# Hybrid decoder layer on one core: the extra 32 rows of an expert multiplied for four weight chunks in one block instead of two

## The chip, the cores and the metric

One core of one Trainium2 chip runs one launch of the kernel. The metric is device microseconds (us) of that launch. Engines: PE is TensorE (PEld its weight loads), DVE VectorE, ACT ScalarE, POOL GpSimd, SP SyncE, whose queue carries most of the loads.

## The reference

One decoder layer over 1024 rows of 1024 columns: pooling and attention, a mixture of experts, a gated projection of `p`, a final norm. The change is in the mixture:

```python
logits = hf @ w_router + b_router            # 1024 rows, 32 experts
topv, topi = lax.top_k(logits, 4)
gates = softmax(topv)
# for each expert e, on the rows xb that chose it:
gu = xb @ w_gate_up[e] + b_gate_up[e]        # 1024 -> 2048
g, u = minimum(gu[:, :1024], 7), clip(gu[:, 1024:], -7, 7)
y = ((u + 1) * g * sigmoid(1.702 * g)) @ w_down[e] + b_down[e]   # 1024 -> 1024
out[row] += gate * y
# behind it
x = x + (p @ w_ple_proj) * sigmoid(rmsnorm(x) @ w_ple_gate)
```

## The kernel before

After the attention part the kernel runs through 32 experts, sorted by their number of rows and interleaved so that large and small ones alternate. Each expert has 128 "main" rows. The 18 large ones, those with `REM[s] = 1` (s counts in processing order), have up to 32 "further" rows as well.

**Chunks.** An expert's weights come as 12 chunks of 1 MB: eight gate-up chunks g0 to g7 (128 rows of `w_gate_up`) and four down chunks d0 to d3 (256 rows of `w_down`). The order is g0..g7 of expert s, then d0..d3 of expert s-1, then g0..g7 of expert s+1, and so on. One pass of the loop (over c, the chunk's number) handles one chunk. Passes are called by their chunk here: "pass g5".

**Main rows.** A chunk lands in a tile `raw`. ACT copies each half to `wh` at reduced precision and DVE forms the rest `wl` (`split`, L104 and L105); pass c splits chunk c+2. PE then makes three products for every 512 columns (`mm3`, L99 to L101), 12 matmuls for a chunk, into `gu` or `d`.

**Further rows.** Their 32 columns fill a quarter of the array's columns, so four products run side by side in the four column groups, in plain float32 straight from `raw`, into a PSUM tile `r` of one buffer. `gu_rem` (L1029) does so for gate-up and `down_rem` (L1085) for down. A group of four products is two instructions each in the trace. Before, `gu_rem` runs in passes g0, g2, g4 and g6 and takes two chunks each time; in g0 it also puts four bias products ahead (L1024). `down_rem` runs in d0 and d2 and takes two chunks. Such a run of instructions is called a block here: six blocks for a large expert, 108 in all.

**What stands between.** Pass g1 transposes the activations of expert s-1 (`a_main`, L979, into `ah` and `al`), g2 the same for its further rows (`a_rem`, L991), g4 and g5 transpose the rows of expert s+1 (`x_main`, L979; `x_rem`, L991), g3 builds one-hot tiles of expert s+2 on DVE, g6 has PE pick its row lists from them (L895, read by small DVE instructions from L916 on). `act_rem` (ACT L1039 and L1040, then DVE) evaluates the gate of the further rows in g6, `act_all` that of the main rows in g7. Output of expert s-2 leaves in g0 (`y_out`).

**Order.** Every engine executes in the order in which the code is written, with waits on semaphores. SP issues the loads in order; a load waits until the former content of its buffer has been split and, for a large expert, multiplied:

```python
for c, (kind, s, k) in enumerate(chunks[:nmain]):
    load_chunk(c + LOADS)          # LOADS = 5, five raw buffers
    ...                            # split(c + 2)
    gu_chunk(s, k, c)
    gu_rem(s, k, c)
```

So the load of chunk c+5 goes into the buffer of chunk c. Behind the loop `p` is read into `pall`, turned and multiplied, and the norms and gates of the eight row tiles follow.

Of the kernel before, what the change touches and what calls it, by code (L numbers as in the profile page):

```python
# [21 lines left out]
D = 1024  # L22
# [49 lines left out]
def layer(ctx, tc, x, p, g_mix, w_in, w_pool, pool_scale, rel_bias, w_out, g_ffn, w_router,  # L72
# [694 lines left out]
    mo_p = tc.tile_pool(name="mo", bufs=1, side="left", reuse_waits="tile")  # L767
    mo = mo_p.__enter__()

    for name in ("al", "ah", "xl", "xh"):  # L770
        mo.tile([128, NK, 128], F32R, name=name, bufs=2)
    for name in ("xr", "atr"):
        mo.tile([128, 256], F32, name=name, bufs=3)
    count(NT - 1)
# [12 lines left out]
    perm2 = rt.tile([128, NE], F32, name="perm2")  # L787
    dve.tensor_scalar(perm2, rank_row, rank, None, op0=OP.is_equal)
    bdb = f3.tile([128, 4, NE], BF, name="bdb")
    bdf = mo.tile([128, D], F32, name="al", bufs=2)[:, :128]  # L790
    with nc.allow_low_precision(reason="zeros and ones"):
        dve.tensor_tensor(bdb, perm2[:, None, :].to_broadcast([128, 4, NE]),
                          maskq[:, :, None].to_broadcast([128, 4, NE]), OP.mult)
# [29 lines left out]

    def onehots(s):
        w = 128 + 128 * REM[s]
        oh = mo.tile([128, NT, 256], BF, name="oh", bufs=1) if s else mo.tile([128, NT, 256], BF, name="ah", bufs=2)
        for i in range(NT):
            dve.tensor_scalar(oh[:, i, :w], slots[:, :w], place[:, i, s:s + 1], None, op0=OP.is_equal)
        S[s]["oh"] = oh
        sel = mo.tile([96, 128], BF, name="sel", bufs=4)  # L830
        dve.tensor_copy(sel, perm2[:96, s:s + 1].to_broadcast([96, 128]))
        S[s]["sel"] = sel
# [32 lines left out]
    def load_chunk(c, after=None, columns=slice(0, 2048)):  # L865
        kind, s, k = chunks[c]
        if c not in raws:
            raws[c] = wp.tile([128, 2048], F32, name="raw", bufs=5)
        if after is not None:
            after.memset(raws[c][:, columns][:, :1], 0.0)  # L870
        if kind in "jp":
            src = w_ple_gate[k * 256:(k + 1) * 256, :] if kind == "p" else w_ple_proj
            sp.dma_start(raws[c].rearrange("p (k c) -> p k c", k=2), src.rearrange("(k p) c -> p k c", p=128))
            return
        if s not in expert:
            expert[s] = sp.value_load(order[0:1, s:s + 1], min_val=0, max_val=NE - 1)
        e = expert[s]
        if kind == "g":
            sp.dma_start(raws[c][:, columns],
                         w_gate_up[ds(e, 1), k * 128:(k + 1) * 128, columns].rearrange("a p c -> p (a c)"))  # L880
        else:
            sp.dma_start(raws[c].rearrange("p (k c) -> p k c", k=2),
                         w_down[ds(e, 1), k * 256:(k + 1) * 256, :].rearrange("a (k p) c -> p (a k) c", p=128))
# [68 lines left out]
    def gates_turned():  # L952

        t = psM.tile([128, 2, 128], F32, name="r", bufs=1)
        for b in range(2):
            pe.transpose(t[:, b, :], gates[:, 4 * b:4 * b + 4, :].rearrange("p i e -> p (i e)"), ident)
        gT = mo.tile([128, D], F32, name="ah", bufs=2)[:, :256]
        act.activation(gT, t.rearrange("p b c -> p (b c)"), AF.Copy)
        t = psM.tile([128, 2, 128], F32, name="r", bufs=1)
        for b in range(2):  # L960
            pe.matmul(t[:, b, :], gT[:, 128 * b:128 * b + 128], bdf, start=True, stop=True)
        return t
# [9 lines left out]

    def turned(src, names):

        hi, lo = (mo.tile([128, NK, 128], F32R, name=n, bufs=2) for n in names)
        for b in range(2):
            t = psM.tile([128, 4, 128], F32, name=f"d{b}", bufs=1)
            for k in range(4):
                pe.transpose(t[:, k, :], src(4 * b + k), ident)  # L979
            split(hi[:, 4 * b:4 * b + 4], lo[:, 4 * b:4 * b + 4], t)  # L980
        return hi, lo
# [33 lines left out]
    def gu_rem(s, k, c):  # L1015


        if not REM[s] or k % 2:
            return
        if k == 0:  # L1020
            S[s]["gur"] = psM.tile([128, 512], F32, name="r", bufs=1)
            table = bgu.rearrange("e (g j c) -> e g j c", g=2, j=4)
            for j in range(4):
                pe.matmul(S[s]["gur"][32 * j:32 * j + 32, :], S[s]["sel"][:, :32], table[:, :, j, :],  # L1024
                          start=True, stop=False)
        for kk in (k, k + 1):
            raw = raws[c + kk - k].rearrange("p (g j c) -> p g j c", g=2, j=4)
            for j in range(4):
                pe.matmul(S[s]["gur"][32 * j:32 * j + 32, :], S[s]["xr"][:, kk, :], raw[:, :, j, :],  # L1029
                          start=False, stop=(kk == NK - 1))  # L1030
# [44 lines left out]
                    k == 0, k == NK - 1)  # L1075

    def down_rem(s, kp, c):
        if not REM[s] or kp % 2:
            return
        if kp == 0:  # L1080
            S[s]["dr"] = psM.tile([128, 256], F32, name="r", bufs=1)
        for k in range(2 * kp, 2 * kp + 4):
            raw = raws[c - kp + k // 2].rearrange("p (k c) -> p k c", k=2)
            for j in range(4):
                pe.matmul(S[s]["dr"][32 * j:32 * j + 32, :], S[s]["atr"][:, k, :],  # L1085
                          raw[:, k % 2, 256 * j:256 * j + 256], start=(k == 0), stop=(k == NK - 1))
# [13 lines left out]
            add_rows(acc4, S[s]["idx", 1], y)  # L1100
        S[s].clear()

    LOADS, SPLITS, TURN0, AT = 5, 4, (4, 7), 8
    load_chunk(0, columns=slice(1024, 2048))

    lists(0, gates=False)
# [33 lines left out]
        split(pT[i][0], pT[i][1], t[:, :2, :])  # L1140

    for c, (kind, s, k) in enumerate(chunks[:nmain]):
        load_chunk(c + LOADS)
        if kind == "g" and k == 0 and s > 1:
            y_out(s - 2)
        if (s, k) != (0, NK - 1):
            for n in range(2 * c + SPLITS, 2 * c + SPLITS + 2):
                split_half(n)
        if kind == "g":
            gu_chunk(s, k, c)  # L1150
            gu_rem(s, k, c)
            if k == NK - 2:
                act_rem(s)
            if k == NK - 1:
                act_all(s)
                if s == 0:
                    for n in range(2 * c + SPLITS, 2 * c + SPLITS + 2):
                        split_half(n)
            if s:
                if k == 1:  # L1160
                    a_main(s - 1)
                if k == 2:
                    a_rem(s - 1)
            if s + 1 < NE:
                if k == 4:
                    x_main(s + 1)
                if k == 5:
                    x_rem(s + 1)
            if s == 0 and k == GK:
                m = psM.tile([128, 2, 2, 6], F32, name="m", bufs=1)  # L1170
                for a in range(2):
                    pick_rows(m[:, a], a, slice(3, 6))
                for a in range(2):
                    slot_gates(m[:, a], a)
                spill_blocks()
            if s == 0 and k == YK:
                for n in range(2):
                    add_rows(acc, rows[:, n:n + 1], ys[n])
            if s + 2 < NE:
                if k == 3:  # L1180
                    onehots(s + 2)
                if k == 6:
                    lists(s + 2)
        else:
            down_chunk(s, k, c)
            down_rem(s, k, c)
            if s == NE - 2 and k == 3:
                pall = mo.tile([128, NT, 256], F32, name="pall", bufs=1)
                act.dma_start(pall, p.rearrange("(i t) c -> t i c", t=128))
                y_out(s)  # L1190
                a_main(NE - 1)
                a_rem(NE - 1)
            if s == NE - 1 and k in (1, 2):
                turn_p(k - 1)
# [84 lines left out]
            dve.scalar_tensor_tensor(r, a, c, r, op0=OP.subtract, op1=OP.mult)  # L1279
        return r  # L1280

    def gain(name, bufs, row):
        g = mo.tile([128, D], F32, name=name, bufs=bufs)
        act.dma_start(g, row_bc(row, D))
        pool.tensor_scalar(g, g, -1.0 / 8192, None, op0=OP.mult)
        return g

    gt = [psM.tile([128, 512], F32, name=f"gu{b}", bufs=1) for b in range(4)]
    gple = gain("oh", 1, g_ple)
    pj, x2, yn, hT = {}, {}, {}, {}  # L1290

    def products(i, n, hi_lo, ws, between=None):
# [15 lines left out]

    def proj(i):
        if i % 2 == 0:  # L1310
            pj[i] = wp.tile([128, 2048], F32, name="raw", bufs=5)
            pj[i], pj[i + 1] = pj[i][:, :D], pj[i][:, D:]
        ps = products(i, 2, pT.pop(i), [parts[2 * nmain + k] for k in range(2)])
        if i + 2 < NT:
            turn_p(i + 2)
        act.activation(pj[i][:, :512], ps[0][0], AF.Copy)
        dve.tensor_copy(pj[i][:, 512:], ps[1][0])

    def load_x2(i):
        name, n = (("xg", 2), ("xg", 2), ("al", 2), ("ah", 2), ("ah", 2))[i % 5]  # L1320
        x2[i] = mo.tile([128, D], F32, name=name, bufs=n)
        sp.dma_start(x2[i], acc[i * 128:(i + 1) * 128, :])

    def squares(i, ss):
# [59 lines left out]
    early(2)  # L1384
    for n in range(2 * nmain + 8, 2 * nmain + 10):
        split_half(n)
    gfin = gain("al", 2, g_final)

    for i in range(NT):
        if i + 4 < NT:  # L1390
# [35 lines left out]
```

## Time and profile before

| | |
|---|---|
| median of 3 runs | 2009.97 us (2009.75 to 2012.18) |
| profiled execution, its own time | 2010.02 us |
| span of its instructions | 2008.3 us |
| PE busy | 1953.4 us, 97% |
| DVE busy | 1502.0 us, 75% |
| ACT busy | 1201.9 us, 60% |
| data moved | 502.18 MB, mean 250 GB/s |

The span is the time from the first to the last profiled instruction; 1.7 us of the run lie outside it. The expert loop takes up about 511 to 1880 us of the span. A matmul's busy time includes its way through the array, so successive ones overlap: from one to the next is read from their starts.

### The profile page before, as it was taken

The numbers are of one execution on the slowest core, as the hardware profiler recorded it, in microseconds if no ns is written. First come the engines' busy times: TensorE is split into PE (matmuls) and PEld (weight loads), VectorE is DVE, ScalarE is ACT, GpSimd is POOL, SyncE is SP. The second block draws the span as 40 slices with busy tenths as digits, with TensorE's granted clock in tenths as the row PEclk, the third lists the DMA queues.
The fourth block names the chain that finished last, engine by engine and source line by source line (L and its number), as shares of the span: only waits on it lengthen the run. The fifth ranks groups of instructions, "written<-read, shape, count | busy, mean of one in ns | idle before, by whom it ended". The sixth has DMA issues, their size and how long they took to land. (4 is left out here: it accounts for less than half of the span.)

```text
span 2008.3 us, 30266 instructions
## 1 busy us (share of the span) xinstructions
PE 1953.4 (97%) x11172; PEld 1429.9 (71%) x11173; DVE 1502.0 (75%) x2464; ACT 1201.9 (60%) x1722; POOL 302.9 (15%) x229
## 2 busy tenths in 40 slices
PE   7999999997999999999999999999999999999998
PEld 6778766775677676677776676776766776766786
DVE  5342575657888797888887887887978787977676
ACT  4222565445667676676676666666766676766533
POOL 0000121302122020212021211120202120201200
PEclk9999999998999999999999999999999999999999
DMA  4421222237898898898897888898987988988711
GB/s 147 126 83 32 85 64 77 93 116 273 324 326 333 293 355 290 304 328 328 307 349 273 310 333 319 312 345 287 353 301 287 335 329 297 351 288 289 241 65 53
DMA packets 117369, 502.18 MB, mean 250 GB/s; under 512 B 12560, under 2 KB 28944, under 8 KB 84576
## 3 DMA queue, kind: packets, MB, share of 16 engines
q1 hardware_dynamic: 99920, 451.46, 59.0%
q0 software_dynamic: 12960, 39.33, 8.6%
q10 hardware_dynamic: 4336, 9.40, 1.5%
q8 instruction: 89, 1.46, 0.3%
q14 instruction: 64, 0.52, 0.1%
HBM read 466.04 MB, written 38.83 MB: 251 GB/s over the span
## 5 line engine op out<-in xcount | busy, mean ns | idle before, releaser
L105 DVE TENSOR_TENSOR wl<-raw,wh 128x1024 fp32r<-128x1024 f32 x778 | 902.9, 1223 | 85.4 <-ACT wh L104 79.3
L104 ACT ACTIVATE wh<-raw 128x1024 fp32r<-128x1024 f32 x778 | 762.5, 1062 | 54.0 <-DMA raw<-in_w_gate_up 30.0
L99 PE MATMUL gu<-wh,xh 128*128 128x512 f32 x1152 | 489.6, 425 | 0.0
L100 PE MATMUL gu<-wl,xh 128*128 128x512 f32 x1152 | 449.6, 390 | 1.9 <-DVE wl L105 1.9
L101 PE MATMUL gu<-wh,xl 128*128 128x512 f32 x1152 | 450.0, 391 | 0.0
L99 PEld LDWEIGHTS gu<-wh,xh 128*128 128x128 f32 x1152 | 218.3, 190 | 65.2 <-issue 17.0
L101 PEld LDWEIGHTS gu<-wh,xl 128*128 128x128 f32 x1152 | 216.3, 188 | 46.7
L100 PEld LDWEIGHTS gu<-wl,xh 128*128 128x128 f32 x1152 | 217.4, 189 | 41.8 <-DVE wl L105 2.6
L100 PE MATMUL d<-wl,ah 128*128 128x512 f32 x512 | 201.3, 393 | 7.8 <-DVE wl L105 7.8
L99 PE MATMUL d<-wh,ah 128*128 128x512 f32 x512 | 203.7, 398 | 0.7 <-DVE al L105 0.7
L1089 POOL DMA_INDIRECT acc<-y,idx x32 | 131.9, 4122 | 446.5 <-ACT y L1095 433.4
L101 PE MATMUL d<-wh,al 128*128 128x512 f32 x512 | 199.2, 389 | 0.0
L906 POOL DMA_INDIRECT xg<-h2d,idx x32 | 52.4, 1638 | 655.5 <-PE gu L101 340.0
L1029 PE MATMUL r<-raw,xr 128*32 128x512 f32 x1152 | 137.9, 597 | 0.0
L104 ACT ACTIVATE xh<-d 128x512 fp32r<-128x512 f32 x80 | 43.6, 596 | 145.2 <-PE d L979 145.2
L99 PEld LDWEIGHTS d<-wh,ah 128*128 128x128 f32 x512 | 96.1, 188 | 34.6 <-issue 12.4
L100 PEld LDWEIGHTS d<-wl,ah 128*128 128x128 f32 x512 | 96.1, 188 | 31.7 <-DVE wl L105 13.6
L101 PEld LDWEIGHTS d<-wh,al 128*128 128x128 f32 x512 | 96.1, 188 | 20.0
L104 ACT ACTIVATE ah<-d 128x512 fp32r<-128x512 f32 x64 | 34.8, 596 | 109.3 <-PE d L979 109.3
L105 DVE TENSOR_TENSOR al<-d,ah 128x512 fp32r<-128x512 f32 x64 | 41.3, 686 | 65.5 <-ACT ah L104 65.5
L1095 ACT ACTIVATE y<-d,gate 128x512 f32<-128x512 f32 x64 | 43.7, 688 | 77.6 <-PE d L101 77.6
L105 DVE TENSOR_TENSOR xl<-d,xh 128x512 fp32r<-128x512 f32 x80 | 51.4, 683 | 51.3 <-ACT xh L104 51.3
(357 smaller groups left out, 2552.1 us busy)
## 6 DMA issues: line engine op xcount, KB each, us to landing
raw<-in_w_gate_up SPq DMA_DIRECT2D x255, 1024.0 KB, 6.3
raw<-in_w_down SPq DMA_DIRECT2D x128, 1024.0 KB, 6.8
wr<-in_w_in SPq DMA_DIRECT2D x16, 512.0 KB, 3.8
rrep<-rvec ACTq DMA_DIRECT2D x8, 576.0 KB, 8.9
xt<-in_x SPq DMA_DIRECT2D x8, 512.0 KB, 3.7
tb<-rrep SPq DMA_DIRECT2D x8, 512.0 KB, 4.7
wor<-in_w_out SPq DMA_DIRECT2D x8, 512.0 KB, 3.7
xr<-in_x SPq DMA_DIRECT2D x8, 512.0 KB, 4.3
```

The lines of the kernel that those rows point to most:

```text
L99: pe.matmul(ps, wh, xh, start=start, stop=False)
L100: pe.matmul(ps, wh, xl, start=False, stop=False)
L101: pe.matmul(ps, wl, xh, start=False, stop=stop)
L104: act.activation(hi, src, AF.Copy)
L105: dve.tensor_tensor(lo, src, hi.bitcast(F32), OP.subtract)
L906: pool.indirect_dma_start(out=xg, out_offset=None, in_=h2d4 if b else h2d, in_offset=bass.IndirectOffsetOnAxis(ap=S[s]["idx", b][:, :1], a ...
L1029: pe.matmul(S[s]["gur"][32 * j:32 * j + 32, :], S[s]["xr"][:, kk, :], raw[:, :, j, :], start=False, stop=(kk == NK - 1))
L1089: pool.indirect_dma_start(out=dst, out_offset=bass.IndirectOffsetOnAxis(ap=idx[:, :1], axis=0), in_=src, in_offset=None, compute_op=OP.add)
L1095: act.activation(y[:, 512 * b:512 * b + 512], S[s]["d"][b], AF.Copy, scale=S[s]["gate", 0])
```

## The change

`gu_rem` now runs in passes g1 and g5 and takes four chunks each time (g0 to g3, g4 to g7), `down_rem` runs in d1 and takes all four. So a large expert has three blocks instead of six; the number of products is the same. Loads run six chunks ahead in seven `raw` buffers: the load of chunk c+6 goes into the buffer of chunk c-1. The room comes from `ah` and `al`, of which there is one buffer each instead of two, and from `pall`, which now takes a `raw` buffer. Three other tiles that lay in `ah` or `al` lie elsewhere: the turned gates at the start in `yr`, the final gain and the rows x2 of tile 4 in the tail in a `raw` buffer called `late`.

```diff
-    for name in ("al", "ah", "xl", "xh"):
-        mo.tile([128, NK, 128], F32R, name=name, bufs=2)
+    for name, n in (("al", 1), ("ah", 1), ("xl", 2), ("xh", 2)):
+        mo.tile([128, NK, 128], F32R, name=name, bufs=n)
...
-            raws[c] = wp.tile([128, 2048], F32, name="raw", bufs=5)
+            raws[c] = wp.tile([128, 2048], F32, name="raw", bufs=7)
...
-        gT = mo.tile([128, D], F32, name="ah", bufs=2)[:, :256]
+        gT = mo.tile([128, 256], F32, name="yr", bufs=2)
...
     def gu_rem(s, k, c):
-        if not REM[s] or k % 2:
+        if not REM[s] or k % 4 != 1:
             return
-        if k == 0:
+        if k == 1:
             S[s]["gur"] = psM.tile([128, 512], F32, name="r", bufs=1)
...
-        for kk in (k, k + 1):
+        for kk in range(k - 1, k + 3):
             raw = raws[c + kk - k].rearrange("p (g j c) -> p g j c", g=2, j=4)
...
     def down_rem(s, kp, c):
-        if not REM[s] or kp % 2:
+        if not REM[s] or kp != 1:
             return
-        if kp == 0:
-            S[s]["dr"] = psM.tile([128, 256], F32, name="r", bufs=1)
-        for k in range(2 * kp, 2 * kp + 4):
+        S[s]["dr"] = psM.tile([128, 256], F32, name="r", bufs=1)
+        for k in range(NK):
...
-    LOADS, SPLITS, TURN0, AT = 5, 4, (4, 7), 8
+    LOADS, SPLITS, TURN0, AT = 6, 4, (4, 7), 8
...
-        load_chunk(c + LOADS)
+        if c + LOADS < len(chunks):
+            load_chunk(c + LOADS)
...
-                pall = mo.tile([128, NT, 256], F32, name="pall", bufs=1)
+                pall = wp.tile([128, 2048], F32, name="raw", bufs=7).rearrange("p (i c) -> p i c", i=NT)
...
-        name, n = (("xg", 2), ("xg", 2), ("al", 2), ("ah", 2), ("ah", 2))[i % 5]
-        x2[i] = mo.tile([128, D], F32, name=name, bufs=n)
+        name, n = (("xg", 2), ("xg", 2), ("al", 1), ("ah", 1), (None, 0))[i % 5]
+        x2[i] = mo.tile([128, D], F32, name=name, bufs=n) if name else late[:, D:]
...
-    gfin = gain("al", 2, g_final)
+    late = wp.tile([128, 2048], F32, name="raw", bufs=7)
+    gfin = gain(late[:, :D], g_final)
```

On PE this moves instructions; on ACT, DVE, POOL and SP the order stays as it was but for one more marker write on POOL at the start. PE in passes g0 to g2 of the first large expert (s = 1), before (`sel` picks the bias, `uc` are the activations of expert 0, an x8 is two groups of four products):

```order
L101 MATMUL gu_4789<-wh,xl 128x512
L1024 LDWEIGHTS sel
L1024 MATMUL r<-bgu,sel 32x512
...
L1029 MATMUL r<-raw,xr 32x512 x8
L99 MATMUL gu_4774<-wh,xh 128x512
...
L101 MATMUL gu_4789<-wh,xl 128x512
L979 MATMUL d_4831<-ident,uc_4743 128x128 x4
L979 MATMUL d_4838<-ident,uc_4747 128x128 x4
L99 MATMUL gu_4774<-wh,xh 128x512
...
L1029 MATMUL r<-raw,xr 32x512 x8
L99 MATMUL gu_4774<-wh,xh 128x512
```

The same passes of the change:

```order
L101 MATMUL gu_4792<-wh,xl 128x512
L1024 LDWEIGHTS sel
L1024 MATMUL r<-bgu,sel 32x512
...
L1029 MATMUL r<-raw,xr 32x512 x16
L979 MATMUL d_4842<-ident,uc_4746 128x128 x4
L979 MATMUL d_4849<-ident,uc_4750 128x128 x4
L99 MATMUL gu_4777<-wh,xh 128x512
```

The blocks of g0 and g2 have become one of twice the length, at the end of g1 and directly ahead of `a_main`'s transposes. PE in passes g4 to g6 of the same expert, before (`xg` are rows of expert 2, L895 the picks):

```order
L101 MATMUL gu_4789<-wh,xl 128x512
L1029 MATMUL r<-raw,xr 32x512 x8
L979 MATMUL d_4940<-ident,xg 128x128 x4
L979 MATMUL d_4947<-ident,xg 128x128 x4
L99 MATMUL gu_4774<-wh,xh 128x512
...
L101 MATMUL gu_4789<-wh,xl 128x512
L1029 MATMUL r<-raw,xr 32x512 x8
L895 LDWEIGHTS oh
L895 MATMUL m<-aux,oh 128x6
```

And of the change, from the end of g5:

```order
L101 MATMUL gu_4792<-wh,xl 128x512
L1029 MATMUL r<-raw,xr 32x512 x16
L99 MATMUL gu_4777<-wh,xh 128x512
...
L101 MATMUL gu_4792<-wh,xl 128x512
L895 LDWEIGHTS oh
L895 MATMUL m<-aux,oh 128x6
```

The second block now stands ahead of the 12 matmuls of g6, which lie between it and the picks.

## Rows read from the trace of the kernel before

**Rows 1.** Windows: us, busy PE, PEld, DVE, ACT, POOL (instructions), clock, DMA share, GB/s.

```profile
511.00:1880.00 1369.00, 1359.19 (x7938) 968.61 (x7936) 1131.91 (x1582) 919.28 (x1154) 227.34 (x95) 1.00 0.87 316
944.00:957.00 13.00, 13.00 (x63) 10.04 (x62) 11.89 (x12) 10.19 (x13) 7.39 (x1) 1.00 1.00 390
```

**Rows 2.** The first of PE's waits, 511 to 1880 us: total, times, longest.

```profile
PE d L100 <- DVE wl L105: 7.8, 13, 1.0
```

**Rows 3.** Timeline of PE and PEld, pass g2 of expert 12: start, length, idle before.

```profile
997.03 0.39 PE L101 MATMUL gu<-wh,xl 128*128 128x512 f32 x1
997.35 1.92 PE L1029 MATMUL r<-raw,xr 128*32 128x512 f32 x16
997.81 0.13 PEld L1029 LDWEIGHTS r<-raw,xr 128*32 128x32 f32 x4 [0.30 <-issue]
998.24 0.13 PEld L1029 LDWEIGHTS r<-raw,xr 128*32 128x32 f32 x4 [0.30 <-issue]
...
999.21 0.50 PE L99 MATMUL gu<-wh,xh 128*128 128x512 f32 x1
...
999.55 0.40 PE L100 MATMUL gu<-wl,xh 128*128 128x512 f32 x1
```

**Rows 4.** Timeline of PE, pass d0 of expert 10: a block of `down_rem`.

```profile
972.34 0.39 PE L101 MATMUL d<-wh,al 128*128 128x512 f32 x1
...
974.86 0.40 PE L100 MATMUL d<-wl,ah 128*128 128x512 f32 x1
```

**Rows 5.** Timeline of PE: transposes behind a block, and behind the plain stream.

```profile
1004.60 0.39 PE L101 MATMUL gu<-wh,xl 128*128 128x512 f32 x1
...
1007.93 0.39 PE L100 MATMUL gu<-wl,xh 128*128 128x512 f32 x1
...
1036.44 0.39 PE L101 MATMUL gu<-wh,xl 128*128 128x512 f32 x1
...
1037.78 0.40 PE L100 MATMUL gu<-wl,xh 128*128 128x512 f32 x1
```

**Rows 6.** Timeline of PE, expert 12: picks, g7, then d0 to d2.

```profile
1015.12 0.55 PE L895 MATMUL m<-aux,oh 128*128 128x6 bf16 x16
...
1018.34 0.39 PE L99 MATMUL d<-wh,ah 128*128 128x512 f32 x1
...
1023.77 0.39 PE L99 MATMUL d<-wh,ah 128*128 128x512 f32 x1
1024.85 0.50 PE L100 MATMUL d<-wl,ah 128*128 128x512 f32 x1 [0.69 <-DVE wl L105]
1025.19 0.39 PE L101 MATMUL d<-wh,al 128*128 128x512 f32 x1
```

**Rows 7.** Timelines of ACT and of DVE over the same stretch.

```profile
1015.25 0.38 ACT L1039 ACTIVATE uc<-r 128x256 f32<-128x256 f32 x1 [2.91 <-PE r L1029]
...
1018.65 0.62 ACT L1039 ACTIVATE uc<-gu 128x512 f32<-128x512 f32 x1
...
1017.01 0.15 DVE L916 TENSOR_REDUCE tok<-m 128x1 f32<-128x2 f32 x1
...
1020.39 0.76 DVE L1042 TENSOR_SCALAR uc<-uc 128x512 f32<-128x512 f32 x2
...
1023.58 9.17 DVE L105 TENSOR_TENSOR wl<-raw,wh 128x1024 fp32r<-128x1024 f32 x8
```

**Rows 8.** Timeline of PE and DVE, expert 11: `a_main` to g4.

```profile
950.88 1.03 PE L979 MATMUL d<-ident,uc 128*128 128x128 f32 x8
953.58 2.36 DVE L105 TENSOR_TENSOR wl<-raw,wh 128x1024 fp32r<-128x1024 f32 x2
957.46 0.39 PE L99 MATMUL gu<-wh,xh 128*128 128x512 f32 x1
```

**Rows 9.** The tile `raw`, 511 to 1880 us: who waited for its loads; issue to landing.

```profile
  DMA raw<-in_w_gate_up: 27.5, 14
...
DMA to landing us min/median/max: 4.6/6.4/12.3
```

More of the change, by code (lines that the diff above doesn't have):

```diff
@@ L789, in layer @@
     bdb = f3.tile([128, 4, NE], BF, name="bdb")
-    bdf = mo.tile([128, D], F32, name="al", bufs=2)[:, :128]
+    bdf = mo.tile([128, D], F32, name="al", bufs=1)[:, :128]
     with nc.allow_low_precision(reason="zeros and ones"):
@@ L825, in onehots @@
         w = 128 + 128 * REM[s]
-        oh = mo.tile([128, NT, 256], BF, name="oh", bufs=1) if s else mo.tile([128, NT, 256], BF, name="ah", bufs=2)
+        oh = mo.tile([128, NT, 256], BF, name="oh", bufs=1) if s else mo.tile([128, NT, 256], BF, name="ah", bufs=1)
         for i in range(NT):
@@ L973, in turned @@
     def turned(src, names):
-        hi, lo = (mo.tile([128, NK, 128], F32R, name=n, bufs=2) for n in names)
+        hi, lo = (mo.tile([128, NK, 128], F32R, name=n, bufs=1 + (n[0] == "x")) for n in names)
         for b in range(2):
@@ L1280, in small_rsqrt, with gain @@
         return r
-    def gain(name, bufs, row):
-        g = mo.tile([128, D], F32, name=name, bufs=bufs)
+    def gain(g, row):
         act.dma_start(g, row_bc(row, D))
@@ L1288, in layer @@
     gt = [psM.tile([128, 512], F32, name=f"gu{b}", bufs=1) for b in range(4)]
-    gple = gain("oh", 1, g_ple)
+    gple = gain(mo.tile([128, D], F32, name="oh", bufs=1), g_ple)
     pj, x2, yn, hT = {}, {}, {}, {}
@@ L1310, in proj @@
         if i % 2 == 0:
-            pj[i] = wp.tile([128, 2048], F32, name="raw", bufs=5)
+            pj[i] = wp.tile([128, 2048], F32, name="raw", bufs=7)
             pj[i], pj[i + 1] = pj[i][:, :D], pj[i][:, D:]
```

## The prediction

> **What bounds the kernel.** I read the windows first: they say which engine fills the stretch that the change touches. In the expert loop PE is busy for 1359 of 1369 us at a granted clock of 1.00; DVE has 1132, ACT 919, and the DMA engines move 316 GB/s at a share of 0.87 [rows 1]. So a microsecond that PE no longer needs is a microsecond of the run, as long as DVE's splits and the loads keep up. Next the list of what PE waited for: at the head of the list stand 13 waits of 7.8 us in sum, all for a `wl` at a down chunk [rows 2]. Last the timeline around single blocks, because a busy share of 97% does not show what changing from one kind of product to another costs.
>
> **What a block costs.** The plain stream takes 5.43 us for the 24 matmuls from the start of d0 to that of d2, 0.226 us each and 2.72 for a chunk [rows 6]. Around a gate-up block the last matmul of the stream starts at 997.03, the block at 997.35, the second matmul behind it at 999.55: 2.52 us, of which two steps of the stream would have taken 0.45. The block costs 2.07. Its groups follow at 0.43 us (997.81, 998.24), four make 1.72, and so 0.35 is paid for the change there and back [rows 3]. A down block has eight groups of half the columns, 0.215 each by the same pace, again 1.72; it costs 2.52 - 0.45 = 2.07 too [rows 4]. So the 0.35 does not grow with the number of groups, and that is what makes merging pay. With transposes behind the block PE needs 3.33 us from the stream's last matmul to the second one after the transposes, without a block 1.34: 1.99, fixed part 0.27, since the transposes break the stream in any case [rows 5].
>
> **What merging saves.** The groups stay, 18 experts times 16 of gate-up and down each; only fixed parts go. Before, of 108 blocks 70 have the stream behind them (18 in g0, 14 in g2, 1 in g4, 2 in g6, 35 down), 38 transposes or picks; I give the picks the price of the transposes. That is 70 x 0.35 + 38 x 0.27 = 34.8 us. After, 54 blocks: 31 with the stream behind (14 in g5, 17 in d1), 23 with transposes (18 `a_main`, 4 `x_rem`, 1 turning `p`): 31 x 0.35 + 23 x 0.27 = 17.1. **Saved: 17.7 us.** At the lower price alone it would be 54 x 0.27 = 14.6, at the upper 18.9. The four bias products keep their place at the head of a block.
>
> **What happens to the 13 waits.** They stand at the second step of d2, where expert s is large and s-1 small. One of them: d2 starts at 1023.77, its `wl` product should follow at 1024.00 and comes at 1024.85; with the refill behind it 1.42 us pass for two steps worth 0.45, a loss of 0.97 for 0.69 of idle time [rows 6]. So 7.8 us of idle time are 7.8 + 13 x 0.28 = 11.4 us of the run. The cause stands on ACT and DVE: in g6 `act_rem` waits 2.91 us for the block that PE has just done (1015.25), DVE's small instructions on the picks start behind it at 1017.01, `act_all`'s clip at 1020.39, and the first `wl` for d2 at 1023.58 [rows 7]. In the change the block is done in g5, a whole pass earlier, and `act_rem` with it. The small instructions then wait for the picks alone, which end at 1015.67 on this scale [rows 6]: up to 1.2 us earlier. The clip needs ACT's second `uc`, which ends at 1019.27 [rows 7]; it could start 1.1 earlier. So `wl` is there by about 1023.7 where it is needed at 1024.0. The margin is 0.3 us, and the sites are not alike (longest wait 1.0, mean 0.6), so I count 9.5 of the 11.4 as gained. With the block gone from g6 and d0, PE reaches d1 and d2 sooner where s is small, too; there the large expert's block now stands between d1 and d2 and gives DVE 3.8 us more for d2, so none of these places becomes tight.
>
> **What is late next.** In g1 the block is twice as long and stands ahead of `a_main`; ACT waits for its transposes, and the splits for g4 are queued behind that wait. A small expert has this sequence without any block: transposes at 950.88, `wl` for g4 complete at 953.58 + 2.36 = 955.94, first product of g4 at 957.46 [rows 8]. Everything from the transposes on is the same after a block, so 1.5 us are left, and PE waits for nothing here. In g5 the doubled block lies ahead of g6, whose splits are done by then.
>
> **Loads.** Now buffers come free in fours, at the end of the blocks in g1, g5 and d1, and four loads start together, 54 times. The first of four is split three passes later at the earliest (behind d1: d2, d3, g0), which is 8.2 us, the fourth six passes later, 16.3. Loads land 6.4 us after issue at the median, with waiting in the queue [rows 9], and when the DMA engines are full they move 390 GB/s [rows 1], 2.69 us for 1 MB: the fourth lands after 14.5. Both have 1.8 us to spare; on top, splits run two passes ahead of PE, so that PE would notice only some 2 us later, at a landing after 10.2: 5.4 us, less 2.36 for DVE's two splits of a chunk [rows 8] and about 1.2 for the one on ACT ahead of them (twice the 0.62 of a tile half as wide [rows 7], an estimate). ACT's waits for gate-up loads, 27.5 us now [rows 9], should shrink. I count nothing for them, as the waits that PE has now go back to ACT's order, not to them. The Trainium skill speaks against this: "DMA: Bandwidth & Descriptors" gives in its specifications a limit of about 358 GB/s of HBM bandwidth for one core. By that figure the fourth load would take 6.4 + 3 x 2.93 = 15.2 us, an estimate from that page, and the spare time would be 1.1. The 390 GB/s of this trace exceeds it, and I go by the trace.
>
> **Edits at no cost.** One buffer of `ah` and `al`: they are written behind transposes that PE does two passes after the last product that read them; were that cover gone, ACT would wait for d3, over by then. `pall` takes the buffer of expert 30's last down chunk, multiplied two passes before; ACT issues it, and what is queued behind, `y_out`, needs d3's end anyway. In the tail x2 is read once the last rows are added, after the last product with `al`. The marker write and a sixth load at the start stand behind five others. None touches PE.
>
> **The sum.** 2010.0 (this execution's own time; the span is 2008.3, and the median of the runs is 2009.97, so it is typical) - 17.7 - 9.5 = **1983 us**.
>
> **Rivals.**
> - *Only the blocks are saved* (0.22). The `wl` for d2 stays late, or another split becomes the last: DVE has 83% of the loop and works in bursts, and 0.3 us is little. 2010 - 17.7 = 1992, from 1988 to 1997.
> - *A merged block costs what two did* (0.05): its groups slow down once the weight loads of a longer run lag. Against it the eight groups of a down block at the same cost as four. If the waits still go, 1999, else 2010.
> - *Bursts come late* (0.05), the case that ends slower. Each 0.1 us beyond a landing at 10.2 us costs 54 x 0.1 = 5.4 us. From 10.7 on it eats the whole gain; at 11.0 the time is 1983 + 43 = 2026. For it: landings up to 12.3 now [rows 9], gathers and scatters of 0.5 MB that fall between. Against it: over the loop the demand rises only to 316 x 1369 / 1342 = 322 GB/s.
> - *More than the sum* (0.06): all 13 waits go and the start gains from the deeper queue, 1976 to 1980.
>
> **How the numbers follow.** The forecast holds with 0.62, from 1979 to 1988. Faster by over 0.2% (4 us; the runs shown lie 0.12% apart, so less can hardly be told) are the forecast, the first and the last rival, and part of the second: 0.92. Within 0.2%: 0.03, the rest of the second. Slower: 0.05, the bursts. The range from 1978 to 1996 leaves out the second and third rival, the lower part of the last and the edge of the first, less than 2 in 10.
>
> **What would show it.** Blocks of 32 and 64 instructions whose groups still follow at 0.43 and 0.215 us, and 54 of them; PE's waits for `wl` at d gone or below 2 us; `act_rem` (ACT L1039 on `r`) no longer in the way of the clip; ACT's waits for loads below 27.5. The forecast is wrong if PE's list shows a new wait on a split or a load, if a block's groups slow down, or if the clock of the loop falls below 1.00: 1.9 us of packed products never lowered it, 3.8 with transposes behind are not in this trace.

## The result and the profile after

The change runs in 1986.08 us (median of 4 runs, 1984.71 to 1987.85), the kernel before on the same chip in 2010.82 (2009.75 to 2012.18). The ratio is 0.9877 with a 95% interval of 0.986 to 0.9894: 1.2% faster, 24.7 us. The prediction was 1983, from 1978 to 1996. The profiled execution took 1986.29 us. Two rows of the page of the changed kernel, its span and the busy times:

```profile
span 1984.5 us, 30275 instructions
...
PE 1933.6 (97%) x11172; PEld 1439.8 (73%) x11173; DVE 1498.1 (75%) x2464; ACT 1200.9 (61%) x1722; POOL 299.3 (15%) x230
```

PE has 19.8 us less busy time at the same number of matmuls, and the share is still 97%. The window over the loop, to be set against [rows 1]:

```profile
511.00:1856.00 1345.00, 1339.49 (x7943) 978.51 (x7941) 1129.60 (x1583) 919.49 (x1155) 223.36 (x95) 1.00 0.86 322
```

The clock stayed at 1.00 and the DMA rate rose to the forecast 322 GB/s. PE's waits in the loop, the list that [rows 2] head:

```profile
PE d L100 <- DVE wl L105: 2.8, 4, 0.7
PE gu L99 <- ACTq L1199: 1.2, 1, 1.2
PE gu L1001 <- DVE uc L1046: 1.0, 1, 1.0
PE d L99 <- DVE al L105: 0.7, 1, 0.7
PE gu L100 <- DVE wl L105: 0.6, 1, 0.6
```

Of the 13 waits for `wl` at d2 ten are gone, all those where the expert after is small. Four are in the list now, where the expert after is large: three that stayed, and one, at `s` = 30, that was not in it before. Next the timelines around the second block of expert 12 (`s` = 12, the expert of [rows 3, 6, 7]), PE and PEld first, then ACT and DVE:

```profile
1000.61 0.39 PE L101 MATMUL gu<-wh,xl 128*128 128x512 f32 x1
1000.93 3.64 PE L1029 MATMUL r<-raw,xr 128*32 128x512 f32 x32
1004.50 0.50 PE L99 MATMUL gu<-wh,xh 128*128 128x512 f32 x1
1004.84 0.40 PE L100 MATMUL gu<-wl,xh 128*128 128x512 f32 x1
...
1010.60 0.39 PE L99 MATMUL d<-wh,ah 128*128 128x512 f32 x1
...
1016.04 0.39 PE L99 MATMUL d<-wh,ah 128*128 128x512 f32 x1
1016.27 0.39 PE L100 MATMUL d<-wl,ah 128*128 128x512 f32 x1
...
1001.38 0.13 PEld L1029 LDWEIGHTS r<-raw,xr 128*32 128x32 f32 x4 [0.30 <-issue]
1001.81 0.13 PEld L1029 LDWEIGHTS r<-raw,xr 128*32 128x32 f32 x4 [0.30 <-issue]
...
1004.63 0.39 ACT L1039 ACTIVATE uc<-r 128x256 f32<-128x256 f32 x1 [1.91 <-PE r L1029]
...
1007.95 0.16 DVE L916 TENSOR_REDUCE tok<-m 128x1 f32<-128x2 f32 x1 [1.41 <-PE m L895]
...
1011.33 0.75 DVE L1042 TENSOR_SCALAR uc<-uc 128x512 f32<-128x512 f32 x2
...
1014.53 3.48 DVE L105 TENSOR_TENSOR wl<-raw,wh 128x1024 fp32r<-128x1024 f32 x3
```

The merged block still has its groups at 0.43 us. From the stream's last matmul (1000.61) to the second one behind the block (1004.84) pass 4.23 us, less 0.45 for two steps is 3.78: less than the 4.14 of two old blocks. `act_rem` is over early, DVE now waits for the picks, and the `wl` for d2 begins at 1014.53: its first half is there 1.22 us later, at 1015.75, 0.5 ahead of the matmul at 1016.27 that needs it and follows without a gap.

The same step where the expert after is large too (`s` = 7), first PE before:

```profile
804.67 0.50 PE L100 MATMUL d<-wl,ah 128*128 128x512 f32 x1 [0.23 <-DVE wl L105]
```

Then a timeline of PE, ACT and DVE of the changed kernel:

```profile
784.55 3.64 PE L1029 MATMUL r<-raw,xr 128*32 128x512 f32 x32
...
800.75 0.50 PE L100 MATMUL d<-wl,ah 128*128 128x512 f32 x1 [0.74 <-DVE wl L105]
...
788.59 0.39 ACT L993 ACTIVATE xr<-m 128x256 f32<-128x256 f32 x1 [4.13 <-PE m L991]
...
789.96 2.36 DVE L105 TENSOR_TENSOR wl<-raw,wh 128x1024 fp32r<-128x1024 f32 x2 [3.67 <-ACT wh L104]
...
799.49 3.48 DVE L105 TENSOR_TENSOR wl<-raw,wh 128x1024 fp32r<-128x1024 f32 x3
```

Here expert 8 has further rows as well. `x_rem` turns them in g5, behind the long block; ACT's copy `xr` waits 4.13 us for that, and the splits, the gates and the small instructions stand in the queues of ACT and DVE behind it. So the wait at d2 stays, and is longer than it was at this place before, 0.74 us of idle time against 0.23. The four waits left stand at `s` = 7, 14, 23 and 30; whether this is their cause is tested below.

### The profile page after: what moved, and what is told of

Same layout as the page of the kernel before. It is cut to its first block, busy times and chain, and to the rows that moved or that the text cites. A ratio compares the mean times of both kernels' runs of the same rounds, so it can differ in the third digit from the quotient of the medians.

```text
span 1984.5 us, 30275 instructions
## 1 busy us (share of the span) xinstructions
PE 1933.6 (97%) x11172; PEld 1439.8 (73%) x11173; DVE 1498.1 (75%) x2464; ACT 1200.9 (61%) x1722; POOL 299.3 (15%) x230
## 5 line engine op out<-in xcount | busy, mean ns | idle before, releaser
L1029 PE MATMUL r<-raw,xr 128*32 128x512 f32 x1152 | 130.5, 594 | 0.0
L99 PEld LDWEIGHTS d<-wh,ah 128*128 128x128 f32 x512 | 96.1, 188 | 27.5 <-ACT wh L104 7.0
L104 ACT ACTIVATE xh<-d 128x512 fp32r<-128x512 f32 x80 | 43.6, 596 | 82.6 <-PE d L979 82.6
L1029 PEld LDWEIGHTS r<-raw,xr 128*32 128x32 f32 x1152 | 34.2, 109 | 73.7 <-issue 72.1
```

What stands on the lines that cost most here:

```text
L99: pe.matmul(ps, wh, xh, start=start, stop=False)
L104: act.activation(hi, src, AF.Copy)
```

## The experiments

Ratios are to the kernel before, timed beside them (medians 2010.5 to 2012.0); "theory" is the account of the prediction until it says otherwise.

**Loads alone.** The seven buffers and the loads six ahead, with the blocks where they were.

```diff
-        if not REM[s] or k % 4 != 1:
+        if not REM[s] or k % 2:
...
-        for kk in range(k - 1, k + 3):
+        for kk in (k, k + 1):
...
-        if not REM[s] or kp != 1:
+        if not REM[s] or kp % 2:
```

> The changed kernel with the blocks of before: two chunks each, in g0, g2, g4, g6, d0 and d2 (108 blocks); seven raw buffers, loads six ahead and the moved tiles stay. Theory (the gain is 54 fixed parts of blocks and the waits that the block in g6 caused): the time of before, 2011 us, within 2; PE keeps its 13 waits for wl at d2 (7.8 us). Rival (the deeper queue of loads gave a part of it): ACT's 30 us of waits for gate-up loads go, the 13 waits with them, and the time falls by 5 to 11, to 2000 to 2006.

Measured: 2011.65 us, ratio 1.0003 (0.9993 to 1.0012). PE's first wait and ACT's only wait for weights in the loads:

```profile
PE d L100 <- DVE wl L105: 7.7, 13, 1.0
```

```profile
ACT wh L104 <- DMA raw<-in_w_gate_up: 2.6, 4, 1.3
```

ACT's waits for loads are nearly gone (27.5 in 14 before, [rows 9]), PE's 13 waits stand unchanged, and so does the time. The loads are worth nothing by themselves. The moved tiles and the single buffers of `ah` and `al` are in this run too, so nor do they cost anything that shows.

**Halves.** The blocks stay in g1, g5 and d1, but each is cut in two round the 12 matmuls of its pass, so that 108 blocks remain and all that moves with the change still moves.

```diff
+            gu_rem(s, k, c, 0)
             gu_chunk(s, k, c)
-            gu_rem(s, k, c)
+            gu_rem(s, k, c, 1)
...
+            down_rem(s, k, c, 0)
             down_chunk(s, k, c)
-            down_rem(s, k, c)
+            down_rem(s, k, c, 1)
```

> The changed kernel with each of its 54 blocks cut in two: one half ahead of the pass's 12 main matmuls, the other where the whole block stood. Loads, buffers and the work of ACT and DVE stay where the change puts them. Theory: 54 more blocks at a fixed part of 0.34 us (2.06 less four groups of 0.43) are 18.5 us, 1986 + 18.5 = 2004.6, or 4 less if the four waits of the changed kernel go, so 2000 to 2005. Rival (a block's price is not in its fixed part, and the gain came from where the blocks stand and how buffers come free): 1986 to 1990.

Measured: 2006.28 us, ratio 0.9976 (0.9966 to 0.9985), 20.2 us more than the change; PE's waits at d2 as in the change:

```profile
PE d L100 <- DVE wl L105: 2.8, 4, 0.7
```

54 more blocks cost 0.37 us each. The median is 1.3 us above what the theory allowed at the upper end (2005); the runs lie between 2004.66 and 2010.58. The number of blocks and the waits are two causes that can be had apart: this run has the gain of the waits and not that of merging.

**Gate late.** The gate of the further rows goes to g7, directly ahead of that of the main rows.

```diff
-            if k == NK - 2:
-                act_rem(s)
             if k == NK - 1:
+                act_rem(s)
                 act_all(s)
```

> The changed kernel with the gate of the further rows (act_rem) evaluated in g7 instead of g6, just ahead of the main rows' gate: DVE then does its 1.2 us behind the picks and not while it waits for them. Theory (the 13 waits went because this work left the chain from the picks to the wl of d2, which has 0.3 to 0.5 us to spare): the chain ends about 1.2 us later, nine waits of some 0.7 come back, each with 0.3 for the refill, and the four that are left get longer: 1986 + 9 or so = 1995 (1991 to 1999). Rival (they went because the loads come earlier): 1986, and no waits come back.

Measured: 1994.75 us, ratio 0.991 (0.9894 to 0.9927). PE's first wait:

```profile
PE d L100 <- DVE wl L105: 8.9, 14, 0.7
```

The waits are back with everything else of the change in place, and so are 8.7 us. What the change gains at d2 it gains because the gate's small chain is out of the way before the main gate begins.

**`x_rem` early.** The further rows of expert s+1 are turned in g4, ahead of the block and not behind it.

```diff
                 if k == 4:
                     x_main(s + 1)
-                if k == 5:
                     x_rem(s + 1)
```

> The changed kernel with x_rem of expert s+1 moved from g5, where it stands behind the long block, to g4, behind x_main. Theory (the four waits of PE that are left, 2.8 us or 4.0 with the refill, stand where s and s+1 are both large: ACT's copy of the turned further rows waits for the whole block, and the splits for d0, the gate and the list work are queued behind it): the four waits go, 1986 - 4 = 1982 (1981 to 1984). Rival (they come from the 1.2 us longer list work or another queue at these places): the four waits stay, 1986.

Measured: 1982.45 us, ratio 0.9849 (0.9833 to 0.9866). No wait for a `wl` at d is left in PE's list, and ACT's wait for `xr` (22.4 us, 18 times, in the change) is gone from its own. 3.6 us at four places, 0.9 each: this was the cause of the waits left.

**Buffers.** Six, five and four `raw` buffers with loads five, five and four ahead; `p` gets a tile of its own.

```diff
-            raws[c] = wp.tile([128, 2048], F32, name="raw", bufs=7)
+            raws[c] = wp.tile([128, 2048], F32, name="raw", bufs=5)
...
-    LOADS, SPLITS, TURN0, AT = 6, 4, (4, 7), 8
+    LOADS, SPLITS, TURN0, AT = 5, 4, (4, 7), 8
...
-                pall = wp.tile([128, 2048], F32, name="raw", bufs=7).rearrange("p (i c) -> p i c", i=NT)
+                pall = mo.tile([128, NT, 256], F32, name="pall", bufs=1)
...
```

The diff is that of five. Six: 

> The changed kernel with six raw buffers and loads five ahead (the load of chunk c+5 goes into the buffer of chunk c-1; pall has a tile of its own again). The first of four loads that a block sets free is then split two passes later instead of three: 5.4 us, and PE would notice some 2 us after that, at a landing after 7.4. Theory (loads have slack): a first load lands 4.6 to 6.4 us after issue, so ACT waits for loads more than now (over 10 us in sum, 2.6 before), PE's waits stay as in the changed kernel, 1986, at most 1989. Rival (bursts are tight already at three passes): 1995 or more.

Five: 

> The changed kernel with five raw buffers, as many as before: the first of four loads is split one pass later, 2.7 us, and PE would notice at a landing after some 4.7. Theory (it is the lead of the loads that decides whether merged blocks pay): with landings of 4.6 to 6.4 us PE waits 0 to 1.7 us behind most of the 54 blocks, 1986 + 20 to 70 = 2006 to 2056, and ACT's waits for loads come to over 100 us. Rival (PE's lead over the splits takes it up, the two more buffers do nothing): 1986 to 1990.

Measured: six 1987.05 us, ratio 0.9877 (0.9862 to 0.9892), as the change; five 1989.36, ratio 0.9896 (0.9878 to 0.9914). The theory's 2006 and more for five did not come: the rival was right. With six, ACT's waits for loads came to 4.1 us in sum, not to the forecast 10 and more. With five, ACT does wait, and PE hardly notices: it is 3 us slower than the change, and the two intervals overlap. With five buffers, ACT's waits for loads and PE's for `wl`:

```profile
ACT wh L104 <- DMA raw<-in_w_gate_up: 103.0, 54, 5.3
...
ACT wh L104 <- DMA raw<-in_w_down: 31.0, 15, 5.9
```

```profile
PE d L100 <- DVE wl L105: 2.9, 4, 0.8
```

The timeline of the same kernel at expert 12's second block, SP's issues (the first of a row), ACT, DVE and PE:

```profile
1000.52 2.11 SPq L882 DMA_DIRECT2D raw<-in_w_down  x3
1003.47 6.77 SPq L879 DMA_DIRECT2D raw<-in_w_gate_up  x3
...
1005.73 2.01 ACT L104 ACTIVATE wh<-raw 128x1024 fp32r<-128x1024 f32 x2 [1.97 <-DMA raw<-in_w_down]
...
1007.53 2.35 DVE L105 TENSOR_TENSOR wl<-raw,wh 128x1024 fp32r<-128x1024 f32 x2
...
999.39 3.64 PE L1029 MATMUL r<-raw,xr 128*32 128x512 f32 x32
...
1011.79 0.39 PE L99 MATMUL d<-wh,ah 128*128 128x512 f32 x1
```

Two things were wrong in the account of the loads. The buffers don't come free together at the block's end (1002.96) but one by one inside it: the first load is issued at 1000.52. And with the queue empty (the share of the DMA engines was 0.03 over the 2.5 us ahead) it lands 5.1 us later, not 6.4, so ACT copies at 1005.73. DVE begins the `wl` at 1007.53, its first half is there 1.22 us later, at 1008.75, and PE needs it for d1 at 1012.0. ACT's wait falls into time in which it had waited for PE: over the run its wait for the transposes of `xh` is 61.5 us here and 82.6 in the change.

The account mended so was tested with one buffer less. In this kernel three of the tail's tiles (`p` and the first two pairs of the projected `p`) have a room of their own, the gain `late` stays in a `raw` buffer, and the last weight chunk is loaded behind the loop.

> The change with four raw buffers and loads four ahead (p's rows, the projected p and the late gain lie in tiles of their own behind the loop, so the tail's loads come a little later). Theory, mended after the run with five buffers: buffers come free one by one inside a block, so the first load of a burst is issued about 2.4 us ahead of the block's end and lands some 5 us later, with an empty queue (1000.52 to 1005.65 in the run with five). With four buffers this load is the one for d0 instead of d1. PE needs its rest at about 1009.3 there; with 1.06 us for the copy and 1.22 for the rest it is ready at 1007.9, so the burst alone stops PE nowhere, and the following loads land 2.5 us apart where PE takes 2.72. But ACT waits for this load ahead of the gate of the further rows, which moves from 1003.1 to about 1007.7, and the gate of the main rows and the splits for d2 behind it move by 1 to 1.5 us. Their margin is 0.4 us where the expert before is small (nine places) and nothing where it is large (four): 13 x 0.6 to 1.5 = 8 to 20 us more than with five buffers. Time 1997 to 2010, PE's waits for wl at d2 at 13 places, ACT's waits for loads above 134 us. Rival A: the lead is still of no weight, 1986 to 1991. Rival B, the reckoning behind the expectation for five buffers (a load lands 6.4 us after the block's end): each of 54 blocks would stop PE by 2.7 us more, 2100 and above.

Measured: 2072.82 us, ratio 1.0294 (1.027 to 1.0317). Neither the mended account nor a rival had this: the mechanism is there, at several times the price. (The places are told apart by the expert after, not by the one before: ten with a small one, four with a large one.) PE's first two waits with four buffers:

```profile
PE d L100 <- DVE wl L105: 44.0, 28, 2.5
PE gu L100 <- DVE wl L105: 9.0, 12, 1.0
```

Its timeline at one second block, with the stream behind it from 1028.69; SP, ACT and PE:

```profile
1025.12 3.64 PE L1029 MATMUL r<-raw,xr 128*32 128x512 f32 x32
...
1026.24 3.02 SPq L882 DMA_DIRECT2D raw<-in_w_down  x4
...
1032.35 2.01 ACT L104 ACTIVATE wh<-raw 128x1024 fp32r<-128x1024 f32 x2 [6.67 <-DMA raw<-in_w_down]
1034.26 0.36 ACT L1039 ACTIVATE uc<-r 128x256 f32<-128x256 f32 x1
...
1039.43 0.50 PE L100 MATMUL d<-wl,ah 128*128 128x512 f32 x1 [1.53 <-DVE wl L105]
...
1044.89 0.80 PE L100 MATMUL d<-wl,ah 128*128 128x512 f32 x1 [2.45 <-DVE wl L105]
```

ACT starts on the first load 6.1 us after its issue here, 5.2 with five buffers. The further gate behind it starts at 1034.26, 5.6 us after the block's end (0.1 after it in the change; the account had 4.7), and then not only the `wl` for d2 is late but that for d1 too: 28 waits, up to 2.5 us each. On top comes the clock. Windows of PE over this stretch (us, busy PE, clock, DMA share, GB/s):

```profile
1036.00:1044.00 8.00, 4.91 (x21) 1.00 1.01 391
1044.50:1047.50 3.00, 2.61 (x6) 0.50 0.56 224
1048.00:1051.00 3.00, 3.00 (x15) 1.00 1.01 404
```

Behind the two waits PE runs for 3 us at 0.50, the lower of its two levels (1.2 of 2.4 GHz). The medians with five and four buffers lie 83 us apart. What waits and clock have of that can be read from the starts of PE's matmuls, which both kernels run in the same order. From expert 2's first bias product to expert 31's the two profiled executions take 1237.3 and 1314.0 us. Of the 76.8 us between them 48.8 are more idle time, 14.7 are steps at 0.50 (with five buffers the clock of this stretch is 1.00 throughout), and 13.3 the refill (the slow steps right behind a wait) and other slower steps.

**Picks early.** `x_rem` early as above, and the picks (L895) at the end of g5, behind the block; the small instructions on them stay in g6.

```diff
+                if k == 5:
+                    picked = picks(s + 2)
                 if k == 6:
-                    lists(s + 2)
+                    lists(s + 2, ps=picked)
```

> The kernel with x_rem in g4, and with the picks of expert s+2 moved from the end of g6 to the end of g5, directly behind the block for a large expert; DVE's list work stays in g6. Theory (a block's fixed part is a break of the stream on both sides, which the picks cause as well): 16 breaks become shared, at about 0.1 us each, and DVE no longer waits for the picks in g6: 1982.4 - 1.6 = 1980.8, (1979.5 to 1982). Rival (picks cost the same wherever they stand): 1982.4.

Measured: 1979.5 us (1977.83 to 1980.79), ratio 0.9838 (0.9825 to 0.9852), the lowest median of all versions. The interval overlaps that of `x_rem` early alone (0.9833 to 0.9866), so by the times the step is not clear of noise. PE's list over the loop, complete:

```profile
PE gu L99 <- ACTq L1204: 1.2, 1, 1.2
PE d L99 <- DVE al L105: 0.7, 1, 0.7
PE gu L100 <- DVE wl L105: 0.7, 1, 0.7
```

By PE's starts the picks cost 0.40 (0.20 for a small successor) behind a block and 0.50 (0.31) in the stream, 1.7 us over 16 places. In the stretch from expert 2 to 31 (as above) the trace has 2.1 us less than `x_rem` early, 1232.9 to 1230.8: 1.6 from the picks and 0.5 from the pace of the other steps (below). The rest of the 3 us between the medians is not explained.

## Why the prediction was right, and what was mis-sized

The stretch from expert 2's first bias product to expert 31's took 1260.04 us before and 1236.97 after. I split the 23.1 us by the starts of all of PE's matmuls (a break is where PE leaves the plain stream for other products and comes back): 14.6 are breaks in the stream, 6.5 waits, and 2.1 the pace of the undisturbed steps, which fell from 228.25 to 227.67 ns (3557 and 3642 steps).

- *A block's cost* (0.35 fixed, groups at 0.43 and 0.215, merging does not stretch them): right. 3.78 us for the merged gate-up block with the stream behind it, 3.79 for the down block. The rival that a merged block costs what two did is out. The Trainium skill, "TensorEngine Tiling (Array Packing)", Tiling Modes, says that changing the tiling mode drains the engine; the trace agrees in so far as a change there and back has a price here, 0.34 to 0.35 us, and the same for 16, 32 and 64 instructions. The page gives no figure, and that the price is this draining no run here shows.
- *17.7 us saved by merging*: a little too much. 48 blocks fewer in that stretch gave 14.6, 0.303 each, so 16.4 for 54. The term that was most off is the picks' price: 0.23 us of a block's fixed part ahead of picks, not the 0.27 of the transposes.
- *The pace* was not in the sum. Behind a break the matmuls follow at 0.232 us at first and come back to 0.227 within about ten steps (means over the stretch before). The 2.1 us of the stretch make about 2.3 for the 54 blocks of the loop. The halves agree: in their trace the undisturbed steps take 228.40 ns and the breaks 0.34 us a block more than in the change; together that is 0.39 a block in this stretch.
- *9.5 us of the 11.4 for the waits*: the mechanism was right, the size was not. `act_rem` out of the way, the small instructions behind the picks alone and the margin of about 0.3 us (0.4 to 0.5 measured) hold at all ten places where the expert after is small. The step that failed is "In g5 the doubled block lies ahead of g6, whose splits are done by then". Where the expert after is large, `x_rem` stands behind that block; ACT's copy of it waits 4.13 us, and the splits behind it are late. The prediction read one place (`s` = 12, the expert after small) for all of them. PE's idle time grew from 0.2 to 0.7 us at `s` = 7, 14 and 23, and at 30 a wait of 0.6 is new, which the prediction had named as a sign of being wrong. 7.4 us were gained; `x_rem` early brings 3.6 more.
- *Loads in time* was right for seven buffers, by a wrong account: it let four loads start together at the block's end and land at the 6.4 us of [rows 9]. They start inside the block (from 1002.05 in the block of 1000.93 that is shown above). The four-buffer run shows that the case which ends slower exists, three buffers lower.
- *Edits at no cost*: no new wait in PE's list answers to `ah`, `al`, `pall` or the tail, which took 129.95 us from the last product with `al` to the end before, and 130.15 after. In the first two experts, though, only 0.3 us were gained where the terms above would give some 1.7. About 1.1 of that is the clock of the profiled execution: it stood at 0.50 already ahead of the loop and stayed there for the loop's first 3.0 us, before for 0.6. Windows of both (before, then after):

```profile
477.60:478.20 0.60, 0.60 (x3) 0.50 (x3) 0.58 (x1) 0.60 (x1) 0.00 (x0) 0.50 1.00 423
478.50:481.50 3.00, 3.00 (x8) 2.06 (x8) 2.25 (x3) 2.89 (x5) 0.38 (x1) 0.50 1.01 421
```

PE also waits for a `wl` at 513.6 (0.6 us) for which it didn't wait before, a second new wait.

So 1983 against 1986 is: 1.3 too much for merging and 2.1 too much for the waits, less 2.3 not counted for the pace, the rest the loop's start and the spread of runs. That the pace made up for two thirds of what was counted too much is luck.

The figure of about 358 GB/s by which the Trainium skill, "DMA: Bandwidth & Descriptors", Specifications, spoke against the bursts does not bound this core: the windows of the four-buffer run have 391 over 8 us and 404 over 3, that at the start of the change's loop 421 over 3. The same page, under Bandwidth, measures 425 for a load of 16 MB on one core, with the pair's other core idle. The 421 come near it.

## What to carry to other kernels

When PE is the bound, look at what changing between kinds of products costs and count the changes: here 54 of them, with the pace behind them, were worth 16 to 20 us without a product less. A block that is moved is also a wait that is moved: for each instruction that now stands behind it, ask which engine waits for it and what is queued there, and ask it for each kind of neighbour, not for one. Buffers that come free early were worth nothing here while a split waited for something else, and much once the last of their lead was gone: between five and four buffers lay 83 us, between seven and five some 3, which is not clear of noise.

## What the runs showed of the hardware

- The matmuls behind a break run slower for about ten steps at a granted clock of 1.00: 232 ns at the second step, 228 at the sixth, 227 from the eleventh (means over the stretch before).
- 3.6 us of packed products with 0.8 us of transposes behind left the clock at 1.00 throughout, which the trace of before could not show; behind two waits of 1.5 and 2.5 us it stood at 0.50, 1.2 GHz, for 3 us.
- Of loads issued 0.9 to 1.2 us apart into an empty queue the first landed after 5.1 us in one place; in another ACT started on it 6.1 us after its issue.
